# A hybrid encoder trunk: TensorE's order of the first stage, from a priority scheduler to a planned, tied weave

## The chip, the cores and the metric

The kernel runs on one core of a Trainium2 chip. A core has five engines with a queue of instructions each: TensorE (PE in the profile; its weight loads stand apart as PEld), VectorE (DVE), ScalarE (ACT), GpSimd (POOL) and SyncE (SP), which here only issues DMAs. The order of each queue is fixed when the program is built; what an instruction has to wait for is told by semaphores. The metric is the device time of one execution in microseconds, lower is better.

## What is computed

A two-layer encoder on 1024 frames of width 1024, all in float32. The part that the change touches is layer 0's mixer: one projection whose columns feed eight RWKV-7 heads and eight heads of chunked band attention.

```python
def rwkv_attention_mixer(h, w_in, mu, ..., rel_bias, w_out):
    proj = h @ w_in
    p_rwkv, q, k, v = jnp.split(proj, [...], axis=-1)
    y_rwkv = rwkv7_group(p_rwkv, mu, ...)
    y_att = chunk_band_attention(q, k, v, rel_bias)
    return jnp.concatenate([y_rwkv, y_att], axis=-1) @ w_out

def step(S, inp):                       # the RWKV recurrence, frame by frame
    r_t, w_t, k_t, v_t, kk_t, a_t = inp
    sa = jnp.einsum('bhij,bhj->bhi', S, -kk_t)
    S = (S * w_t[:, :, None, :] + sa[..., None] * (kk_t * a_t)[:, :, None, :]
         + v_t[..., None] * k_t[:, :, None, :])
    y = jnp.einsum('bhij,bhj->bhi', S, r_t)

for layer in range(DEPTH):              # DEPTH = 2
    h = rmsnorm(x, mix_norms[layer])
    x = x + (rwkv_attention_mixer(h, ...) if layer % 2 == 0 else conformer_conv(h, ...))
    x = x + sq_relu_mlp(rmsnorm(x, g_ffn), up, down)
```

## The kernel before

**Dense work.** Activations lie with channels on the 128 partitions and 512 frames (one half `h` of the sequence) in the free dimension. A dense step multiplies a 128x128 weight tile with a 128x512 tile. Float32 operands are split into a high and a low part, and three matmuls (lines 270 to 272) take the place of one: high by high, high by low, low by high. One output tile takes 8 x 3 of them. In the order of the program the dense work is: `w_in` for half 0, `w_in` for half 1, `w_out` and layer 0's MLP for half 0, and then layer 1 and the rest. The weights are loaded by SP, cast by ACT (214) and subtracted by DVE (215), under the priority "support".

**RWKV.** The recurrence is made in chunks of 64 frames. A unit is two heads by 256 frames (four chunks); there are 8 units for each half, 16 in all. `prep` mixes r, k and v from the projections that were written to DRAM, makes decays, normalises k (sums over heads at 439, spread back at 446) and forms the chunk matrices `g` by eight matmuls of 64x128 tiles (546), masked by DVE (549). The diagonal 16x16 blocks of `g` then have to be inverted. They are gathered by eight small DMAs into DRAM (`msc`, 557) and two back (`nb`, 562), DVE inverts them in about twenty short steps (574 to 585), two DMAs write the result (`xsc`, 592), eight read it back as diagonal blocks (`xdt`, 599), and DVE transposes them (605). The first matmul that uses that is 611; three more rounds (623) make the inverses of the whole chunks. `stacks` transposes operands (640, 645), `chain` carries the state through the four chunks with three dependent matmuls each (668, 672, 678), every one followed by copies on DVE and ACT, and `finish` normalises the output (702 to 720). Below, "the inversion loop" is what lies between a unit's last matmul of 546 and the end of its transpose 605.

**Attention.** For each pair of heads and each tile of 128 queries: scores (797, 799), softmax on DVE and ACT (801 to 810), transposes (819), and probabilities by values (826).

**What sets the order.** The kernel emits these streams one after the other under priorities (`At("support")` first, then "mixer", "attn", "dense"), and a list scheduler at build time places each engine's instructions by priority among what it takes to be ready. So TensorE's dense steps fill what the streams leave. The RWKV and attention of half 0 share TensorE with `w_in` of half 1, those of half 1 with `w_out` and the MLP of half 0. PSUM, TensorE's output memory, is parted into `d` (2 banks, dense), `w` (2), `v` (1), `c` (1, the chain) and `a` (2, attention).

Of the kernel before, what the change touches and what calls it, by code (L numbers as in the profile page):

```python
# [14 lines left out]
P = 128  # L15
# [38 lines left out]
LINE = 32  # L54

# [6 lines left out]
def encoder_trunk(ctx: ExitStack, tc: tile.TileContext, x, vecs, consts, ext, w2a2, g2, w_in, w_out,  # L62
# [15 lines left out]
    deferred = []  # L78

    def psum(tag):  # L80
        return ps[tag].tile([P, T], F32, tag=tag, name=tag)

# [68 lines left out]

    def tmp(tag="t1"):
        return dpool.tile([P, T], F32, tag=tag, name=tag)
# [16 lines left out]
    class Stat:  # L170
# [12 lines left out]
        def sums(self, eps_col=0):  # L183
            q = psum("o" if wide[0] and self.ps == "d" else self.ps)
            with At("dense") if wide[0] else nullcontext():
                for j in range(4):
                    nc.tensor.matmul(q[:, j : j + 1], self.acc[:, j * P : (j + 1) * P], ones[:, 0:1], start=True, stop=True)
# [6 lines left out]
        def spread(self):  # L194
            q, c = self.part
            with At("dense") if wide[0] else nullcontext():
                for j in range(4):
                    nc.tensor.transpose(q[:, j * P : (j + 1) * P], c[:, j : j + 1].to_broadcast([P, P]), ident)
            self.r = self.pool.tile([P, T], F32, tag=self.pre + "rstd", name="rstd", bufs=1)
            nc.scalar.copy(self.r[:], q[:])  # L200
# [22 lines left out]
    def gemm(w, row0, mts, rhs, evac, st=None, first=(), taper=False, after=None, halves=False):  # L223
# [28 lines left out]
        for i, (grp, cols) in enumerate(units):  # L252
# [3 lines left out]
            for k in range(KT):  # L256
# [10 lines left out]
                with At("dense"):  # L267
                    for q, parts in zip(qs, ws):
                        hi, lo = (a[:, k % KH, :] for a in parts[k // KH])
                        nc.tensor.matmul(q[:, cols], hi, xh[:, cols], start=(k == 0), stop=False)  # L270
                        nc.tensor.matmul(q[:, cols], hi, xl[:, cols], start=False, stop=False)  # L271
                        nc.tensor.matmul(q[:, cols], lo, xh[:, cols], start=False, stop=(k == KT - 1))  # L272
# [6 lines left out]
            if after is not None:  # L279
                late_m += [(m, cols) for m in grp]  # L280
        if late_m:
            deferred.append(tail)

    IN_ORDER = [12, 13] + [t for j in range(4) for t in (j, 4 + j, 8 + j)] + list(range(14, 22))


    def load_x(h, xrp, out=None):
# [17 lines left out]
        for k in range(KT):  # L305
            q = psum("w" if k % 2 else "a") if h == 0 else psum("w")
            for t in range(4):
                nc.tensor.transpose(q[:, t * P : (t + 1) * P], raws[t][:, k * P : (k + 1) * P], ident)
# [26 lines left out]
    def w_in_gemm(h, rhs, st, first=()):  # L335
        def evac(m, q, cols):
# [14 lines left out]
            else:  # L351
                nc.gpsimd.dma_start(pd[m][:, ts], s[:])

        gemm(w_in, 0, IN_ORDER, rhs, evac, st, first)
        qs = [psum(tag) for tag in SPARE]
        for k in range(KT):
            with boost():
                hi, lo = (a[:].rearrange("p a b -> p (a b)")
                          for a in weight_part(w_in[k * P : (k + 1) * P, V0 * P : V0 * P + RW], RW))
            xh, xl = rhs[k]  # L360
            with At("dense"):
                for t, q in enumerate(qs):
                    ts = slice(t * P, (t + 1) * P)
                    nc.tensor.matmul(q[:], xh[:, ts], hi, start=(k == 0), stop=False)
                    nc.tensor.matmul(q[:], xl[:, ts], hi, start=False, stop=False)
                    nc.tensor.matmul(q[:], xh[:, ts], lo, start=False, stop=(k == KT - 1))
        with boost():
            for t, q in enumerate(qs):
                s = tmp("t1")
                nc.scalar.activation(s[:], q[:], AF.Copy, scale=st.part[1][:, t : t + 1])  # L370
                nc.gpsimd.dma_start(vd[h * T + t * P : h * T + (t + 1) * P, :], s[:])


    def rwkv(h, rp, nbuf):
# [12 lines left out]
        for i in range(n + 2):  # L387
            gens = []
            if i >= 2:
                gens.append(units[i - 2][2]())  # L390
            if 1 <= i <= n:
                gens.append(units[i - 1][1]())
            if i < n:
                gens.append(units[i][0]())
            while gens:
                for g in list(gens):
                    try:
                        next(g)
                    except StopIteration:
                        gens.remove(g)  # L400

    def rwkv_block(tb, rp, nbuf, keep):
# [28 lines left out]
        def vbank():  # L431
            return psum("v")[:, 0:RT]
# [4 lines left out]
        def head_sums(q, src):  # L437
            for b in range(RT // P):
                nc.tensor.matmul(q[:, 2 * b : 2 * b + 2], src[:, b * P : (b + 1) * P], bones[:, 0 : C + 1 : C],
# [3 lines left out]
        def head_spread(q, r, wide):  # L443
            nc.scalar.copy(wide[:].rearrange("p (h c) -> p h c", c=C), r[:].unsqueeze(2).to_broadcast([P, 4, C]))
            for b in range(RT // P):
                nc.tensor.transpose(q[:, b * P : (b + 1) * P], wide[:, b * P : (b + 1) * P], ident)
# [16 lines left out]
        def prep(hp, u):  # L463
            if not lora_in:
                shared()
                yield
# [5 lines left out]
            vp = rp.tile([P, RT + 2 * C], F32, tag="vp", name="vp", bufs=nbuf - 1)  # L472
            nc.gpsimd.memset(vp[:, 0:C], 0.0)
            nc.gpsimd.memset(vp[:, RT + C : RT + 2 * C], 0.0)
            mix(8 + hp, vp[:, C : RT + C])
            yield
            wps = rbank()
            aps = rbank()
            for i, q in enumerate((wps, aps)):
                nc.tensor.matmul(q, lora[i][:, cs], lora_in[i][:], start=True, stop=False)  # L480
                nc.tensor.matmul(q, lora[2 + i][:, cs], lora_in[i][:], start=False, stop=True)
# [14 lines left out]
            yield  # L496
            ksq = e()
            nc.scalar.activation(ksq[:], k[:], AF.Square, scale=v("k_k", hp))
            sps = rbank()
            inv = head_sums(sps, ksq)  # L500
            nc.scalar.activation(inv[:], sps[:, 0:4], AF.Sqrt)
            nc.vector.tensor_scalar(inv[:], inv[:], 1e-12, None, op0=ALU.max)
            nc.vector.reciprocal(out=inv[:], in_=inv[:])
            yield
            head_spread(sps, inv, e())
            yield
# [21 lines left out]
            yield  # L528
# [4 lines left out]
            nc.tensor.matmul(bps, bones, bon[:], start=True, stop=True)  # L533
            bv = rp.tile([P, RT], F32, tag="bv", name="bv", bufs=nbuf)
            nc.vector.tensor_tensor(out=bv[:], in0=bps, in1=vp[:, C : RT + C], op=ALU.mult)

            yield
            g = rp.tile([P, NCH, 2, 2, C], F32, tag="g", name="g", bufs=nbuf)
            mask = con("mask").rearrange("p (k t) -> p k t", k=2).unsqueeze(1).to_broadcast([P, 4, 2, C])
            for q4 in range(NCH // 4):  # L540
                mb = [bank(), bank()]
                for j in range(4):
                    c = 4 * q4 + j
                    for hd in range(2):
                        s = slice(64 * hd, 64 * hd + 64)
                        nc.tensor.matmul(mb[hd][:, j * P : (j + 1) * P], bk[s, c, :], ar[s, c, :],  # L546
# [18 lines left out]
            u.update(hp=hp, g=g, ar=ar, bk=bk, vp=vp, dc=dc, bv=bv, nb=nb)  # L565

        def invert(u):
            hp, g, nb = u["hp"], u["g"], u["nb"]
# [10 lines left out]
            for r in range(8):  # L579
# [7 lines left out]
                if r == 4:  # L587
                    yield
            xsc = dram.tile([2, 16, 16, 16], F32, tag=f"xsc{tb}{hp}", name="xsc")
            x0 = xsc[:]  # L590
            for hd in range(2):
                nc.sync.dma_start(bass.AP(tensor=x0.tensor, offset=x0.offset + 4096 * hd,
                                          ap=[[64, 4], [256, 16], [1, 64]]),
                                  xi[C * hd : C * hd + C, :, :].rearrange("p a b -> p (a b)"))
            xd16 = keep["xdt"]
# [11 lines left out]
            hs = [slice(0, C), slice(C, P)]  # L607
            tq = vbank()
            for c in range(NCH):
                for hd, s in enumerate(hs):  # L610
                    nc.tensor.matmul(tq[s, c * C : c * C + C], g[s, c, 0, hd, :], xn[s, c * C : c * C + C],
                                     start=True, stop=True)
            yield
# [5 lines left out]
            for i in range(3):  # L619
                uq = vbank()  # L620
                for c in range(NCH):
                    for s in hs:
                        nc.tensor.matmul(uq[s, c * C : c * C + C], at[s, c * C : c * C + C], rhs[s, c, :],  # L623
                                         start=True, stop=True)
                yield
                if i < 2:
                    rhs = blk(e("e2", 2)[:])
                    nc.vector.tensor_tensor(out=rhs, in0=blk(uq), in1=xd16, op=ALU.add)
            xt = u["xt"] = keep["xt", hp % 2]
            for hd, s in enumerate(hs):  # L630
                nc.vector.tensor_tensor(out=xt[s, :, hd, :], in0=blk(uq)[s, :, :], in1=xd16[s, :, :], op=ALU.add)

# [544 lines left out]
```

## Time and profile before

| | |
|---|---|
| median of three timed runs | 2471.99 us (2471.95 to 2474.72) |
| the profiled execution | 2471.67 us |
| its span, first to last instruction | 2469.9 us |
| TensorE busy / weight loads / DVE / ACT / POOL | 99% / 80% / 69% / 49% / 5% of the span |
| mean granted TensorE clock | 0.998 |
| last matmul of the RWKV and attention streams starts at | 872.8 us |
| matmul rows in the trace | 12828 |

The profile comes from one execution. A row of a timeline has the start in us, the duration in us, the engine, the line, the operation with its output tile and its inputs, shapes, a count where equal rows were merged, and in brackets how long the engine had been idle and what ended that. Matmuls overlap: a dense matmul lasts 0.39 us from its start to its end, and the next one starts 0.23 us after it. So TensorE counts as busy while it waits for less than the overlap, and starts of neighbouring rows say more than busy shares. A float32 matmul that is not split or a transpose shows as two rows; the program has 11338 matmuls for those 12828 rows. Every line number in these rows is that of the kernel before; in the kernel after, all matmuls have the line of a helper, and are told apart by the names of their tiles.

### The profile page before, as it was taken

To read this page: it belongs to the slowest core of one execution; us is meant where nothing else is said; L and a number is where in the kernel's file an instruction comes from. 1 tells how busy PE (TensorE), PEld (TensorE's weight loads), DVE (VectorE), ACT (ScalarE), POOL (GpSimd) and SP (SyncE) were. 2 spreads that over 40 slices of the span, in tenths; PEclk is the share of its full clock that TensorE was granted. 3 is DMA by queue.
4 is the path that set the end of the run, shared out by engine and by line. 5 is a ranking of instruction groups with operands and counts; after the bars stand their busy time and mean duration, and the time that the engine had idled before them with its cause. 6 is when DMAs were issued, how large, how long until landed. Compare 5 with 4: busy or idle time off the path is not lost.

```text
span 2469.9 us, 37195 instructions
## 1 busy us (share of the span) xinstructions
PE 2436.1 (99%) x12828; PEld 1967.3 (80%) x12828; DVE 1715.7 (69%) x3575; ACT 1199.1 (49%) x2308; POOL 114.0 (5%) x283
## 2 busy tenths in 40 slices
PE   8999999999999999999999999999999999999998
PEld 6777777777777788888888888888888888888887
DVE  5688875688877534459999946599998475444444
ACT  5557766577766733343443235434432365433334
POOL 1110111100000000001000000000000000000000
PEclk9999999999999999999999999999999999999999
DMA  8554434643233233373333333533333334333332
GB/s 270 169 151 129 129 104 137 204 116 104 84 105 92 75 96 95 99 213 95 95 96 100 95 98 93 163 98 95 94 95 101 94 103 149 99 94 97 100 94 69
DMA packets 476460, 283.36 MB, mean 115 GB/s; under 512 B 44512, under 2 KB 453472, under 8 KB 476272
## 3 DMA queue, kind: packets, MB, share of 16 engines
q1 hardware_dynamic: 466080, 250.25, 34.9%
q0 software_dynamic: 9152, 29.36, 3.3%
q8 instruction: 101, 1.65, 0.3%
q10 hardware_dynamic: 1040, 1.38, 0.2%
q14 instruction: 87, 0.71, 0.1%
HBM read 247.31 MB, written 36.72 MB: 115 GB/s over the span
## 4 chain that ended last, share of the span: by engine, by line
PE 91%; DVE 3%; DMA 3%; ACT 2%; issue 1%; SPq 0%; ACTq 0%; DVEq 0%
PE d L270 25%; PE d L271 25%; PE d L272 25%; PE a L826 2%; PE w L546 1%; PE v L623 1%; PE a L819 1%; PE a L797 1%; PE c L678 1%; PE c L668 1%; DVE wl L215 1%; PE c L672 1%; DMA pt<-pd 1%; PE a L799 1%; DMA nb<-msc 1%
## 5 line engine op out<-in xcount | busy, mean ns | idle before, releaser
L214 ACT CAST wh<-wr 128x512 fp32r<-128x512 f32 x744 | 461.0, 621 | 949.9 <-PE d L271 866.2
L270 PE MATMUL d<-xh,wh 128*128 128x512 f32 x1872 | 741.9, 396 | 0.5 <-ACT wh L214 0.5
L272 PE MATMUL d<-xh,wl 128*128 128x512 f32 x1872 | 738.3, 395 | 0.9 <-DVE wl L215 0.9
L271 PE MATMUL d<-xl,wh 128*128 128x512 f32 x1872 | 739.2, 395 | 0.0
L215 DVE TENSOR_TENSOR wl<-wr,wh 128x512 fp32r<-128x512 f32 x744 | 503.1, 687 | 218.6 <-ACT wh L214 165.2
L272 PEld LDWEIGHTS d<-xh,wl 128*128 128x128 f32 x1872 | 352.8, 188 | 70.8 <-DVE wl L215 1.6
L270 PEld LDWEIGHTS d<-xh,wh 128*128 128x128 f32 x1872 | 352.8, 189 | 70.4 <-issue 1.3
L271 PEld LDWEIGHTS d<-xl,wh 128*128 128x128 f32 x1872 | 353.1, 189 | 68.5 <-issue 1.2
L270 PE MATMUL d<-mh,wh 128*128 128x512 f32 (+1 forms) x1040 | 403.7, 388 | 0.0
L271 PE MATMUL d<-ml,wh 128*128 128x512 f32 (+1 forms) x1040 | 403.5, 388 | 0.0
L272 PE MATMUL d<-mh,wl 128*128 128x512 f32 (+1 forms) x1040 | 403.2, 388 | 0.0
L949 DVE SCALAR_TENSOR_TENSOR cv<-u,dwt,cv 128x512 f32<-128x512 f32 x480 | 333.1, 751 | 0.7
L270 PEld LDWEIGHTS d<-mh,wh 128*128 128x128 f32 x1040 | 195.6, 188 | 38.1 <-issue 0.2
L272 PEld LDWEIGHTS d<-mh,wl 128*128 128x128 f32 x1040 | 195.5, 188 | 38.2
L271 PEld LDWEIGHTS d<-ml,wh 128*128 128x128 f32 x1040 | 195.4, 188 | 38.1
L848 DVE TENSOR_TENSOR x<-d,x 128x512 f32<-128x512 f32 (+1 forms) x146 | 97.8, 682 | 154.7 <-PE d L272 154.5
L890 DVE SCALAR_TENSOR_TENSOR t<-d,rstd 128x512 f32<-128x512 f32 x128 | 86.6, 689 | 114.9 <-PE d L272 112.2
L896 DVE TENSOR_TENSOR ml<-t,mh 128x512 fp32r<-128x512 f32 x128 | 88.1, 690 | 20.7 <-ACT mh L894 18.0
L892 ACT ACTIVATE t<-t 128x512 f32<-128x512 f32 x128 | 80.1, 626 | 15.8 <-DVE t L890 15.2
L894 ACT ACTIVATE mh<-t 128x512 fp32r<-128x512 f32 x128 | 78.9, 616 | 0.0
L181 DVE TENSOR_TENSOR acc<-acc,t 128x512 f32<-128x512 f32 (+1 forms) x86 | 58.0, 675 | 9.0 <-ACT t L180 8.7
L677 ACT ACTIVATE sd<-vs,dc 64x64 f32<-64x64 f32 x128 | 44.2, 345 | 31.2 <-DVE vs L681 23.3
(273 smaller groups left out, 2407.3 us busy)
## 6 DMA issues: line engine op xcount, KB each, us to landing
wr<-in_up_dram SPq DMA_DIRECT2D x256, 256.0 KB
wr<-in_dn_dram SPq DMA_DIRECT2D x256, 256.0 KB
wr<-in_w_in_dram SPq DMA_DIRECT2D x104, 256.0 KB
wr<-in_pw_dram SPq DMA_DIRECT2D x96, 256.0 KB
wr<-in_w_out_dram SPq DMA_DIRECT2D x32, 256.0 KB
pd<-t POOLq DMA_DIRECT2D x28, 256.0 KB, 2.6
x<-xd SPq DMA_DIRECT2D x24, 256.0 KB
pt<-pd SPq DMA_DIRECT2D x42, 128.5 KB
```

The source lines that it names most:

```text
L181: nc.vector.tensor_tensor(out=self.acc[:, cols], in0=self.acc[:, cols], in1=sq[:, cols], op=ALU.add)
L214: nc.scalar.copy(hi[:], raw[:])
L215: nc.vector.tensor_tensor(out=lo[:], in0=raw[:], in1=hi[:].bitcast(F32), op=ALU.subtract)
L270: nc.tensor.matmul(q[:, cols], hi, xh[:, cols], start=(k == 0), stop=False)
L271: nc.tensor.matmul(q[:, cols], hi, xl[:, cols], start=False, stop=False)
L272: nc.tensor.matmul(q[:, cols], lo, xh[:, cols], start=False, stop=(k == KT - 1))
L848: nc.vector.tensor_tensor(out=xs[m][:, cols], in0=q[:, cols], in1=xs[m][:, cols], op=ALU.add)
L890: nc.vector.scalar_tensor_tensor(out=t[:], in0=q[:], scalar=0.0, in1=rstd[:], op0=ALU.max, op1=ALU.mult)
L892: nc.scalar.activation(sq[:], t[:], AF.Square)
L894: nc.scalar.activation(hi[:], t[:], AF.Square)
L896: nc.vector.tensor_tensor(out=lo[:], in0=sq[:], in1=hi[:].bitcast(F32), op=ALU.subtract)
L949: nc.vector.scalar_tensor_tensor(out=c[:], in0=u[:, tap : tap + T], scalar=dw(tap), in1=c[:], op0=ALU.mult, op1=ALU.add)
```

## The change

TensorE's order in the stage that holds RWKV and attention is no longer found by the scheduler. Every matmul goes through a helper that adds a nominal duration to a planned clock, `pe["now"]`, and, while `strict` is on, ties the instruction to the one before it by a dependency that costs no semaphore and only fixes the order. The dense work becomes a generator that yields after every group of three matmuls. RWKV's `prep`, `invert`, `stacks`, `chain` and `finish` and the attention become five plus one jobs, each a generator that yields a `Need`: so many planned us after now, so many free `w` banks, perhaps a condition on another job. `weave` takes a dense group, and then lets every job go whose need is met on the planned clock; `drain` runs the jobs without dense work.

With it come smaller edits. PSUM's `v` bank joins `w` (3 banks). The inversion's DVE steps and its `xsc` DMAs move from `invert` into the end of `prep`, and `invert` begins with the `xdt` DMAs; its first matmul stands at least 25 planned us after the unit's `g` matmuls. In `prep` the sums for k's norm come before the decays, and v is loaded later. The second transposes of `stacks` become eight 64-column matmuls with an identity, and the transpose and copy of line 602 go. Half 0's `w_in` is split: five tiles before, then three tiles, the value part, and the rest in another order within the weave. Outside of the weave (layer 1 and on) the same work is emitted as before.

```diff
+    pe = {"now": 0.0, "last": None, "strict": False, "w": [0.0] * 3, "held": [], "shape": None}
...
+    def issued(ins, us, shape):
+        pe["now"] += us + (SWITCH if shape != pe["shape"] else 0.0)
+        pe["shape"] = shape
+        if pe["strict"]:
+            if pe["last"] is not None:
+                tc.add_manual_dep(ins.ins, pe["last"].name,
+                                  mybir.DependencyInfo(mybir.DependencyClass.NoSync, mybir.DependencyReason.DATA),
+                                  reason="order of TensorE")
+            pe["last"] = ins.ins
...
+    class Job:
...
+        def ready(self):
+            w = self.want
+            if w.cond is not None:
+                if not w.cond():
+                    return False
+                self.want = w = Need(w.after, w.shape, w.banks, None, w.hold)
+                self.at = max(self.at, pe["now"] + w.after)
+            return pe["now"] >= self.at and sum(t <= pe["now"] for t in pe["w"]) >= w.banks
...
+    def weave(dense, jobs):
+
+        pe["strict"] = True
+        value = None
+        while True:
+            if all(j.done for j in jobs):
+                pe["strict"] = False
+            try:
+                next(dense)
+            except StopIteration as e:
+                value = e.value
+                break
+            pump(jobs)
+        return value
...
+        return [
+            Job("mixer", job("chain", lambda i, hp: was("invert", i) and was("stacks", i)), lead=True),
+            Job("mixer", job("stacks", lambda i, hp: was("prep", i) and was("chain", i - (nbuf - 1)))),
+            Job("mixer", job("invert", lambda i, hp: was("prep", i))),
+            Job("mixer", job("prep", lambda i, hp: all((h, m) in have for m in srcs(hp)))),
+            Job("mixer", job("finish", lambda i, hp: was("chain", i))),
+        ]
...
-            u.update(hp=hp, g=g, ar=ar, bk=bk, vp=vp, dc=dc, bv=bv, nb=nb)
-
-        def invert(u):
-            hp, g, nb = u["hp"], u["g"], u["nb"]
...
+            u.update(hp=hp, g=g, ar=ar, bk=bk, vp=vp, dc=dc, bv=bv, xsc=xsc, made=pe["now"])
+
+        def invert(u, ui, was):
+            hp, g, xsc = u["hp"], u["g"], u["xsc"]
...
-            vl = psum("v")[:, 0:P]
-            nc.tensor.transpose(vl, u["vp"][:, NCH * C : NCH * C + P], ident)
-            nc.scalar.copy(u["vs"][:, :, 1, NCH - 1, :], vl[:, C:P].unsqueeze(1).to_broadcast([P, 2, C]))
...
+            yield Need(max(6.5, u["made"] + 25.0 - pe["now"]), 1, 1)
...
-        def chain(u):
+        def chain(u, ui, was):
+            link = 2.1
...
-                nc.tensor.matmul(zp, g[:, c, 0, :, :].rearrange("p h t -> p (h t)"), sv[:, :, c, :], start=True, stop=True)
+                matmul(zp, g[:, c, 0, :, :].rearrange("p h t -> p (h t)"), sv[:, :, c, :], start=True, stop=True)
...
+                yield Need(link)
...
+            jobs.append(Job("attn", attention(0, ap)))
+
+            def dense():
+                yield from w_in_gemm(0, ra, sa)
+                for what in w_in_gemm(1, reload_x(1, lp), sb):
+                    if what == "value":
+                        drain(jobs, jobs[-1:])
+                    yield
+
+            weave(dense(), jobs)
+            drain(jobs)
```

**TensorE, where the inversion loop ends.** These are rows of TensorE's order around the first matmuls that use a unit's inverse (the row with `g` and 64x64), for the fifth unit. `d` is a dense output, `c` the chain's bank, `a` attention's, `v` and `w` the other streams' banks. Before:

```order
L270 MATMUL d<-xh,wh 128x512
L271 MATMUL d<-xl,wh 128x512
L272 MATMUL d<-xh,wl 128x512
L611 MATMUL v<-e_2661,g 64x64 x8
L439 MATMUL w<-cst,e 128x2 x2
```

And now:

```order
L105 MATMUL d<-xh,wl 128x512
L105 MATMUL c<-zs,xt_682 128x64
L105 MATMUL w<-e_3406,g 64x64 x8
L105 MATMUL d<-xh,wh 128x512
L105 MATMUL d<-xl,wh 128x512
L105 MATMUL d<-xh,wl 128x512
L105 MATMUL w<-ar,bk 128x128 x8
```

The streams now stand between groups of exactly three dense matmuls. What moved is the distance: between a unit's last `w<-ar,bk` matmul and its first with `g` and 64x64 there stood 62 to 140 dense matmuls before, 96 in the mean of the 16 units (82 for this one), and now 54 to 96, 70 in the mean (72 for this one). All matmuls counted, it was 149 to 232 and is 107 to 145. Over the whole program, neighbours of different kinds (split dense work or not, another size of the array's tile) were 1045 and are 872.

**DVE, where the inversion starts.** These are DVE's rows from the masks of the first unit (`g<-w,cst`) to the first step of its inversion (`fold<-nb`), with `wl` a weight's low part. Before:

```order
L549 TENSOR_TENSOR g<-w,cst 128x8x64 x2
L422 SCALAR_TENSOR_TENSOR vp<-pt,vec,e 128x256
L663 COPY vs<-sfin 64x64 x2
L343 TENSOR_TENSOR t_776<-d,rstd 128x512
L215 TENSOR_TENSOR wl<-wr,wh 128x512
L490 SCALAR_TENSOR_TENSOR dx<-wx,cst 128x260
L493 RECIPROCAL e<-dx 128x256
```

Now:

```order
L684 TENSOR_TENSOR g<-w,cst 128x8x64 x2
L324 TENSOR_TENSOR wl<-wr,wh 128x512
L799 COPY vs<-sfin 64x64 x2
L614 TENSOR_SCALAR hs<-hs 128x4
L615 RECIPROCAL hs<-hs 128x4
L324 TENSOR_TENSOR wl<-wr,wh 128x512 x2
L705 TENSOR_TENSOR fold<-nb 128x128
```

Before, five more rows follow until that unit's `fold<-nb`, so that eleven lie between; now five do. From a unit's masks to its transpose 605, DVE has 92 instructions in the mean of the 16 units before (68 to 109) and 65 now (50 to 76); with the median duration of each kind in the trace of before these are 35.0 and 24.5 us of DVE work. Of that, what stands from `fold<-nb` to the last step of the inversion is 16.1 us before and 11.7 us now (7.0 to 15.9).

More of the change, by code (lines that the diff above doesn't have):

```diff
@@ L54 @@
 LINE = 32
+PER_COL = 0.443e-3
+SWITCH = 0.09
 def whole(n):
@@ new lines, in encoder_trunk, with __init__, pump, open_ @@
+    class Need:
+        def __init__(self, after, shape=0, banks=0, cond=None, hold=1.4):
+            self.after, self.shape, self.banks, self.cond, self.hold = after, shape, banks, cond, hold
+    def pump(jobs, force=False):
+        def open_():
+            return [j for j in jobs if not j.done and j.ready()]
+        some = open_()
+        if not some:
+            return False
+        if not force and not any(j.lead for j in some):
+            soon = any(j.lead and not j.done and j.want.cond is None and j.at - pe["now"] < 1.4 for j in jobs)
+            if soon and all(pe["now"] - j.at < 2.0 for j in some):
+                return False
+        free = sum(t <= pe["now"] for t in pe["w"])
+        take = []
+        for j in some:
+            if j.want.banks <= free:
+                free -= j.want.banks
+                take.append(j)
+        for j in sorted(take, key=lambda j: j.want.shape):
+            j.go()
+        return True
@@ new lines, in weave, with drain @@
+    def weave(dense, jobs):
[4 more added lines that the diff above has]
+                pe["strict"] = False
+            try:
+                next(dense)
[4 more added lines that the diff above has]
+        return value
+    def drain(jobs, some=None):
+        while not all(j.done for j in some or jobs):
+            if not pump(jobs, True):
+                pe["now"] += 0.1
@@ L152, in tmp, with run @@
+    def run(gen):
+        while True:
+            try:
+                next(gen)
+            except StopIteration as e:
+                return e.value
     def tmp(tag="t1"):
@@ L352, in evac, with value_part @@
                 nc.gpsimd.dma_start(pd[m][:, ts], s[:])
[L354 to L361, printed above, removed]
+            have.add((h, m))
+        def value_part():
+            qs = [psum(tag) for tag in SPARE]
+            for k in range(KT):
+                with boost():
+                    hi, lo = (a[:].rearrange("p a b -> p (a b)")
+                              for a in weight_part(w_in[k * P : (k + 1) * P, V0 * P : V0 * P + RW], RW))
+                xh, xl = rhs[k]
@@ new lines, in value_part @@
+                    yield
+            with boost():
+                for t, q in enumerate(qs):
+                    s = tmp("t1")
+                    nc.scalar.activation(s[:], q[:], AF.Copy, scale=st.part[1][:, t : t + 1])
+                    nc.gpsimd.dma_start(vd[h * T + t * P : h * T + (t + 1) * P, :], s[:])
+            ready_v.add(h)
+        if ahead:
+            yield from gemm(w_in, 0, ahead, rhs, evac, st, first)
+            return
+        if h == 0:
+            yield from gemm(w_in, 0, IN_ORDER[5:8], rhs, evac, st)
+            yield from value_part()
+            yield from gemm(w_in, 0, LATE_ORDER, rhs, evac, st)
+        else:
+            yield from gemm(w_in, 0, IN_ORDER, rhs, evac, st)
+            yield "value"
+            yield from value_part()
@@ L386, in rwkv, with job @@
         n = len(units)
[L387 to L400, printed above, removed]
+        done = set()
+        was = lambda what, i: i < 0 or (what, i) in done
+        def job(what, cond):
+            for i in range(n):
+                hp = i % 4
+                yield Need(0.0, 0, 0, lambda: cond(i, hp))
+                yield from units[i][what](i, was)
+                done.add((what, i))
+        srcs = lambda hp: [12, 13, hp, 4 + hp, 8 + hp]
+        return [
[5 more added lines that the diff above has]
+        ]
     def rwkv_block(tb, rp, nbuf, keep):
@@ L618, in invert @@
             rhs = xd16
-            for i in range(3):
+            for j in range(3):
+                yield Need(1.8, 1, 1, (lambda: was("chain", ui - 2)) if j == 2 else None)
                 uq = vbank()
@@ L853, in evac @@
                 last(m, cols)
-        gemm(w, row0, range(KT), rhs, evac, taper=taper, after=after, halves=halves)
+        yield from gemm(w, row0, range(KT), rhs, evac, taper=taper, after=after, halves=halves)
     def norm_collect(xs, gname):
@@ L935, in evac @@
                 us[j] = u
-        gemm(pw1, 0, [m for j in range(KT) for m in (j, KT + j)], rhs, evac, st)
+        yield from gemm(pw1, 0, [m for j in range(KT) for m in (j, KT + j)], rhs, evac, st)
         return us
```

253 lines of the change are left out of this document (145 added, 108 removed).

## The prediction

> **What bounds the kernel now.** I read the windows first, to see which stage has anything to give.
>
> ```profile
> 100.00:450.00 350.00, 346.60 (x2393) 262.51 (x2392) 262.29 (x793) 229.99 (x522) 42.26 (x102) 1.00 0.44 131
> 450.00:880.00 430.00, 421.89 (x2952) 327.11 (x2951) 321.00 (x967) 301.60 (x641) 29.43 (x92) 1.00 0.38 109
> 880.00:2470.00 1590.00, 1581.19 (x7090) 1310.62 (x7088) 1076.79 (x1715) 614.74 (x1049) 26.59 (x32) 1.00 0.36 105
> ```
>
> The columns are the window, its length, and the busy time and rows of PE, PEld, DVE, ACT and POOL, then the granted clock. From 880 us on TensorE runs dense work alone; nothing there is touched. In the two windows before it, which hold RWKV and attention, TensorE is idle for 350 - 346.60 + 430 - 421.89 = 11.5 us. So the kernel is bound by TensorE from end to end, and whatever makes TensorE wait or work longer in the woven stage is added to the end, one for one. Busy time hides short waits, though, so I went on to the starts of neighbouring rows, in TensorE's timeline.
>
> ```profile
> 603.39 0.33 PE L819 MATMUL a<-cst,pt 128*128 128x128 f32 x1
> 603.48 0.49 PE L271 MATMUL d<-xl,wh 128*128 128x512 f32 x1
> 603.80 0.60 PE L819 MATMUL a<-cst,pt 128*128 128x128 f32 x4
> 604.16 0.47 PE L272 MATMUL d<-xh,wl 128*128 128x512 f32 x1
> 604.47 0.39 PE L270 MATMUL d<-xh,wh 128*128 128x512 f32 x1
> 604.70 0.39 PE L271 MATMUL d<-xl,wh 128*128 128x512 f32 x1
> ```
>
> A dense matmul behind another one takes 0.23 us (604.47 to 604.70). Behind a transpose it takes 0.31 to 0.32 (603.48 to 603.80, 604.16 to 604.47). **A change of kind costs 0.09 us.** If every row of the two windows is given the usual step of its shape and of its neighbours' kinds, the 2393 + 2952 rows come to 736 us of the 780: TensorE waits there for 44 us at the most, and for 11.5 at the least.
>
> Then I looked for the wait that the change makes tight, and took the quickest of the 16 inversion loops, that of the last unit. TensorE, DVE and SP, each from its own timeline:
>
> ```profile
> 785.67 0.93 PE L546 MATMUL w<-ar,bk 64*128 64x128 f32 x6
> 816.92 0.68 PE L611 MATMUL v<-e,g 64*64 64x64 f32 x16
> ```
>
> ```profile
> 786.64 0.69 DVE L549 TENSOR_TENSOR g<-w,cst 128x512 f32<-128x512 f32 x1 [1.96 <-PE w L546]
> 794.92 0.38 DVE L574 TENSOR_TENSOR fold<-nb 128x128 f32<-128x128 f32 x1 [0.70 <-DMA nb<-msc]
> 803.71 0.29 DVE L585 TENSOR_REDUCE xi<-pr 128x8 f32<-128x128 f32 x1
> 815.76 0.45 DVE L605 STREAM_TRANSPOSE e<-xdt 128x256 f32<-128x256 f32 x1
> ```
>
> ```profile
> 784.36 4.71 SPq L557 DMA_DIRECT2D msc<-g  x8
> 791.73 0.56 SPq L562 DMA_DIRECT2D nb<-msc  x1
> 804.02 1.18 SPq L592 DMA_DIRECT2D xsc<-xi  x2
> 806.74 2.75 SPq L599 DMA_DIRECT2D xdt<-xsc  x6
> 811.48 0.97 SPq L599 DMA_DIRECT2D xdt<-xsc  x2
> ```
>
> The last matmul of `g` starts at 786.3, the masked `g` is there at 787.3, the gathered blocks 7.6 us later (DVE waited for their DMA at 794.92), the inversion ends at 804.0, and the transpose at 816.2. That is **29.9 us** with nothing wasted but DVE's queue. Another unit, the eighth:
>
> ```profile
> 346.49 1.16 PE L546 MATMUL w<-ar,bk 64*128 64x128 f32 x8
> 383.50 0.45 DVE L605 STREAM_TRANSPOSE e<-xdt 128x256 f32<-128x256 f32 x1
> ```
>
> Its last matmul starts at 347.4 and its transpose ends at 383.9, 36.6 us. Over the 16 units (the first ends at 131.4, the last is the one above) it is 29.9 to 48.6 us, 38.6 in the mean. TensorE hardly waits for it before:
>
> ```profile
> L611 PE MATMUL v<-e,g 64*64 64x64 f32 x256 | 11.2, 224 | 1.9 <-DVE e L605 1.5 <-DVE st L809 0.2
> L672 PE MATMUL c<-zs,xt 128*128 128x64 f32 x128 | 24.8, 275 | 1.3 <-ACT zs L671 0.8
> ```
>
> The group of 611 shows 1.9 us of idle time in all, since the scheduler put it 96 dense matmuls behind `g`. The new order puts it 70 behind.
>
> **The change part by part.** I add up against the profiled execution, 2471.67 us (span 2469.9 and 1.8 around it), which is the median of the timed runs to 0.4 us.
>
> Changes of kind: 1045 become 872, 173 x 0.09 = 15.6 us less. The 16 transposes of 602 go too, at about 0.1 each between dense steps; the eight narrow matmuls that replace four transposes in `stacks` I take for equal. Together **-17 us**, all on the path, since TensorE is the bound.
>
> Waits of the old order: between 11.5 and 44 us stand there. The links of the chain give an idea of what the plan can save. In a quick one TensorE comes back 1.4 us later:
>
> ```profile
> 845.85 0.38 PE L668 MATMUL c<-vs,g 128*128 128x128 f32 x2
> 847.22 0.43 PE L672 MATMUL c<-zs,xt 128*128 128x64 f32 x2 [0.30 <-ACT zs L671]
> ```
>
> The plan asks for 2.1 us, nine dense steps. That covers a quick link, but not one whose copy stands behind 0.7 us operations on DVE and ACT. So I let **24 us** of the 44 go, and keep 20. The other waits stated (2.4 in `finish`, 4.5 before the spread, 8 before the bonus) are of the same sort and are in this term.
>
> The inversion loop: between the last `g` matmul and the first use stand, in the new order, 54 to 96 dense matmuls and 11 to 85 others. For the last unit: 96 x 0.227 = 21.8, eleven chain matmuls for about 2.0 (0.2 each, 0.1 for the narrow ones), and the kind changes' 23 x 0.09, part of which the small rows' overlap gives back: 25 us. Done so for all 16 it is 22.5 to 26.6, 24.8 in the mean. So the planned 25 us are what TensorE has to do there, if nothing else waits. The loop needs: 1.0 to mask, 7.6 to gather, the inversion, and 8.5 or more to return. The last is from SP's rows, two `xsc` issues 1.2, 1.5 until the first lands, eight `xdt` issues, then their landing and the transpose.
>
> ```profile
> L599 SPq DMA_DIRECT2D xdt<-xsc x128: 303/424/1879, 121.8 to 812.0; - x128
> ```
>
> The row gives minimum, median and maximum of an issue: 8 x 0.424 = 3.4, and with landing (about 2, as from `xsc` to `xdt`) and 0.45 for the transpose 8.5. The inversion is 11.7 us of DVE work in the new order (other streams' steps stand between); in the old one 16.1 us of work took 14.9 us, so 10.8. Sum 1.0 + 7.6 + 10.8 + 8.5 = 27.9, and 29 with some of SP's queue. **TensorE waits 29 - 24.8, about 4 us.** What is queued behind: all of TensorE, for its order is tied, dense steps too, and so DVE's evacuations and, through the weights' buffers, SP. For two units the wait of the one before falls into their own room, so 14 x 4 = **+56 us**. The ends: none, if the loop shrinks to 25; (38.6 - 24.8) x 16 = 220 if it stays as slow as before. I take the value near the quickest row, since DVE's work in the loop falls from 35.0 to 24.5 us.
>
> The clock: this shows what follows a wait of that size.
>
> ```profile
> 69.77 0.39 PE L270 MATMUL d<-xh,wh 128*128 128x512 f32 x1
> 74.31 0.55 PE L480 MATMUL w<-xl,lora 128*128 128x256 f32 x1 [4.15 <-DVE xl L461]
> 75.73 0.63 PE L272 MATMUL d<-xh,wl 128*128 128x512 f32 x1
> 76.15 0.63 PE L270 MATMUL d<-xh,wh 128*128 128x512 f32 x1
> 79.99 0.41 PE L270 MATMUL d<-xh,wh 128*128 128x512 f32 x1
> 80.25 0.39 PE L271 MATMUL d<-xl,wh 128*128 128x512 f32 x1
> ```
>
> ```profile
> 75.00:80.00 5.00, 5.00 (x15) 3.94 (x14) 2.02 (x5) 0.92 (x3) 0.82 (x3) 0.50 0.59 181
> ```
>
> After 4.15 us of idle time TensorE has half its clock until about 80: a dense step takes 0.43 instead of 0.23, ten of them lose 2 us, and 2.3 with the small ones ahead. Seven of the 16 loops come out with waits over 4 us, so 7 x 2.3 = **+16 us**.
>
> The Trainium skill, "TensorE: Matmul & The Clock Gate", section "Why this matters for your kernels", asks for no idle gap over about 3 us between bursts, since a window of idleness halves the clock. The trace agrees for 4.15 us. By that rule taken strictly, 14 waits instead of 7 would pay, 16 us more; by the row alone the sum stands as it is. It speaks against tying all of TensorE to one late operand.
>
> Sum: -17 - 24 + 56 + 16 = +31, so 2471.67 + 31 = **2503 us**.
>
> **The rivals.** *The loop fits its room* (the plan works). It needs 25 us instead of 29: that takes an inversion of 7 us, as five of the 16 orders on DVE allow (7.0 to 8.7 us of work), in all units. Then only -17 and -11.5 to -44 are left, 2411 to 2443; with 10 us for new short waits, 2440. This ends faster, and it decides at a loop of about 27 us, where the waits (14 x 2 = 28, with no clock loss) still leave -13. For it speaks that DVE's queue is shorter; against it the DMA parts, 16 us of SP issues and landings that the change doesn't shorten.
>
> *Gain and wait cancel*: a loop of 27.5 to 28, 14 x 3 = 42 against 41; 2472. The chain waits less long then, and no clock is lost.
>
> *The loop stays long*: SP's in-order queue holds weights that wait for buffers between `xsc` and `xdt` (at 811.48 two `xdt` issues stand 2 us behind the six others). At 33 us the wait is 8.2, x 15 = 123, plus 15 x 2.3 = 34, less 41: 2588.
>
> That the order isn't what the plan says is excluded: the rows of the new order stand in groups of three dense matmuls.
>
> **How the numbers follow.** Forecast (loop waits, 2480 to 2540): 0.52. Loop fits: 0.28. Cancel: 0.11. Long: 0.09. The range that leaves out 2 in 10 drops the lower third of the second case and most of the last: 2432 to 2555. The forecast alone would be 2480 to 2540. A change of 0.2%, 5 us, is about what a measurement of this kernel can tell from none. Faster: 0.28 and a little of the cancelling case, 0.30; same 0.09; slower 0.61.
>
> **What would show it.** In the profile after, the group with output `w`, inputs `e,g` and 64x64 should head TensorE's idle times, with some 50 us, ended by the transpose on DVE, and the granted clock in 100 to 880 should fall below 1.00. The rows from the last `w<-ar,bk` to that group should show 28 to 30 us. The chain's three groups should keep their idle times or lose some. If that group has under 10 us, the loop step is wrong, and the time is near 2440. If other groups head the idle times (loads of `pt`, softmax), I missed a wait. A second stage that is longer than 1590 us from the last stream's matmul on would contradict the claim that nothing there is touched.

## The result, and the profile after

The changed kernel takes **2595.1 us** (median of four runs, 2590.9 to 2597.3) where the kernel before took 2472.0 (2471.3 to 2474.7) on the same chip: a ratio of 1.049, 95% interval 1.048 to 1.051. It is slower by 123 us. The direction was forecast, the size was not: 2503 was predicted and the range ended at 2555.

From the page of the kernel after, the busy times and the granted clock in 40 slices:

```profile
PE 2434.3 (94%) x13004; PEld 1992.5 (77%) x13004; DVE 1717.5 (66%) x3575; ACT 1203.7 (46%) x2294; POOL 107.0 (4%) x251
PEclk9988899999999999999999999999999999999999
```

The windows of the kernel after, with the columns of the windows before:

```profile
100.00:450.00 350.00, 295.75 (x2067) 235.34 (x2067) 227.96 (x669) 195.17 (x424) 33.97 (x82) 0.92 0.40 117
450.00:880.00 430.00, 375.37 (x2540) 304.81 (x2536) 270.06 (x780) 260.42 (x536) 26.87 (x65) 0.94 0.36 106
880.00:1000.00 120.00, 105.66 (x784) 85.89 (x783) 80.18 (x252) 75.95 (x157) 4.73 (x13) 0.99 0.30 85
1000.00:1200.00 200.00, 192.17 (x1056) 156.40 (x1057) 101.07 (x203) 77.58 (x153) 6.40 (x18) 0.99 0.33 95
1200.00:2590.00 1390.00, 1386.13 (x6230) 1149.16 (x6228) 988.55 (x1583) 544.30 (x935) 21.32 (x27) 1.00 0.35 104
```

In the two windows up to 880 us TensorE now idles 54.3 + 54.6 = 109 us, where it was 11.5, and starts 4607 rows instead of 5345. The streams no longer end there: their last matmul starts at 1113.4 us instead of 872.8, and from 880 to 1200 us TensorE idles another 14.3 + 7.8 = 22 us. Over the whole span it idles 2595.1 - 2434.3 = 161 us, where it was 34. The clock is granted at 0.92 and 0.94 instead of 1.00, worth at most 0.08 x 350 + 0.06 x 430 = 54 us of TensorE's time, part of which it idled anyway. No other engine is busier in these two windows: DVE and ACT are busy for less time too. From 1200 us on, nothing is lost. So TensorE waits, and the view of TensorE's waits in the kernel after says for what (the line after the arrow is the releaser's; then total, times, longest):

```profile
PE a L109 <- ACT pt L953: 36.9, 14, 6.3
PE w L105 <- DVE e L735: 23.1, 9, 5.9
PE c L105 <- DVE sfin L819: 17.4, 16, 2.3
PE a L109 <- ACT pT L964: 12.8, 4, 6.3
PE a L105 <- DVE st L944: 9.6, 5, 5.4
PE w L105 <- ACT e L610: 8.5, 1, 8.5
PE c L105 <- ACT zs L807: 6.9, 9, 2.4
```

The groups of TensorE in the kernel after (busy, mean ns of one, then the idle time ahead and its releasers) say the same:

```profile
L109 PE MATMUL a<-cst,pt 128*128 128x128 f32 x240 | 42.6, 301 | 49.7 <-ACT pt L953 36.9 <-ACT pT L964 12.8
L105 PE MATMUL w<-e,g 64*64 64x64 f32 x256 | 11.8, 236 | 23.1 <-DVE e L735 23.1
```

The inversion (`e`, 735) stands second with 23.1 us. First is the softmax, which the prediction's sum didn't price: 36.9 + 12.8 us ahead of the transposes of the probabilities. Third is the state's update (819), behind which the change states no wait after the chain's last chunk.

How the waits hang together is seen in one inversion loop of the kernel after, that of the eleventh unit. TensorE:

```profile
730.28 1.16 PE L105 MATMUL w<-ar,bk 64*128 64x128 f32 x16
...
742.42 0.27 PE L105 MATMUL a<-kk,ql 128*128 128x128 f32 x1
...
747.79 0.74 PE L109 MATMUL a<-cst,pt 128*128 128x128 f32 x5
...
750.23 0.39 PE L105 MATMUL d<-mh,wl 128*128 128x512 f32 x1
756.94 1.33 PE L109 MATMUL a<-cst,pt 128*128 128x128 f32 x5 [6.32 <-ACT pT L964]
757.92 0.78 PE L105 MATMUL d<-mh,wh 128*128 128x512 f32 x1
758.50 0.63 PE L105 MATMUL d<-ml,wh 128*128 128x512 f32 x1
758.92 0.63 PE L105 MATMUL d<-mh,wl 128*128 128x512 f32 x1
...
764.21 0.68 PE L105 MATMUL w<-e,g 64*64 64x64 f32 x16
```

The last `g` matmul starts at 731.2 and the first use at 764.2, 33.0 us later. There TensorE waits for nothing, though the loop is 8 us longer than its planned 25: it has stood for 6.3 us at five transposes on the way, and then runs dense steps of 0.42 us (758.50 to 758.92) where the steps ahead of the stop took 0.23. One stop has served two late operands. DVE, ACT and SP in the same stretch, each from its own timeline:

```profile
742.41 0.28 DVE L705 TENSOR_TENSOR fold<-nb 128x128 f32<-128x128 f32 x1
747.04 0.29 DVE L944 CUSTOM_DVE_ANT_0 pt<-a,bias 128x128 f32<-128x128 f32 x1
749.39 0.14 DVE L950 TENSOR_SCALAR st<-st 128x1 f32<-128x1 f32 x1
752.93 0.29 DVE L716 TENSOR_REDUCE xi<-pr 128x8 f32<-128x128 f32 x1
761.44 0.44 DVE L735 STREAM_TRANSPOSE e<-xdt 128x256 f32<-128x256 f32 x1
```

```profile
751.18 1.28 ACT L951 ACT_TABLE_LOAD   x1
752.48 0.83 ACT L951 ACTIVATE pt<-pt,st 128x640 f32<-128x640 f32 x1
753.72 0.83 ACT L953 ACTIVATE pt<-pt,st 128x640 f32<-128x640 f32 x1
756.32 0.57 ACT L964 COPY pT<-a 128x512 f32<-128x512 f32 x1
```

```profile
736.86 0.57 SPq L697 DMA_DIRECT2D nb<-msc  x1
738.76 0.56 SPq L697 DMA_DIRECT2D nb<-msc  x1
753.25 1.18 SPq L721 DMA_DIRECT2D xsc<-xi  x2
755.10 3.61 SPq L732 DMA_DIRECT2D xdt<-xsc  x8
```

The last scores of that tile's second head start at 742.4. DVE takes them at 747.0, since steps of another unit's `prep`, the inversion's own and two of the dense work stand in its queue; the maximum is there at 749.5; ACT, after other streams' work, loads a table and takes the exponential at 752.5; the copy of the first head's transposes (964), which ends TensorE's wait, stands behind all that on ACT and starts at 756.3, 8 us after those transposes. The plan states 1.6 us between them and the second head's. No operation in these two queues lasts over 1.3 us on the way. The planner counts only TensorE's own durations, and a queue like this isn't in the waits it states.

The loop's own parts here: 731.2 to 742.4 for mask and gather (SP's last issue of `nb` is done at 739.3, and the first step on it starts 3.1 us later), to 753.2 for the inversion, to 761.9 for the way back (SP issues until 758.7). Over the 16 units the means are 12.0, 10.3 and 10.1 us, 32.4 together, and the way from `g` to the first use is 29.5 to 37.8 us, 33.2 in the mean.

### The profile page after: what moved, and what is told of

Its sections match the earlier page's. It is cut to its first block, busy times and chain, and to the rows that moved or that the text cites. A ratio compares the mean times of both kernels' runs of the same rounds, so it can differ in the third digit from the quotient of the medians.

```text
span 2595.1 us, 37406 instructions
## 1 busy us (share of the span) xinstructions
PE 2434.3 (94%) x13004; PEld 1992.5 (77%) x13004; DVE 1717.5 (66%) x3575; ACT 1203.7 (46%) x2294; POOL 107.0 (4%) x251
## 3 DMA queue, kind: packets, MB, share of 16 engines
q1 hardware_dynamic: 466080, 250.25, 33.2%
## 4 chain that ended last, share of the span: by engine, by line
PE 59%; DVE 0%; ACT 0%; issue 0%; ACTq 0%; DVEq 0%
PE d L105 58%; PE o L109 0%; PE w L105 0%; PE c L105 0%; PE o L105 0%; PE w L109 0%; DVE wl L324 0%; ACT u L1169 0%; DVE t L1035 0%; DVE sfin L819 0%; ACT t L1037 0%; ACT wh L323 0%; ACTq L1330 0%; ACT mh L1039 0%; DVE x L993 0%
## 5 line engine op out<-in xcount | busy, mean ns | idle before, releaser
L105 PE MATMUL d<-xh,wh 128*128 128x512 f32 x1872 | 768.0, 410 | 1.3 <-ACT wh L323 1.3
L105 PEld LDWEIGHTS d<-xh,wl 128*128 128x128 f32 x1872 | 358.0, 191 | 79.6 <-DVE wl L324 1.8
L105 PEld LDWEIGHTS d<-xh,wh 128*128 128x128 f32 x1872 | 359.0, 192 | 77.9 <-issue 4.7
L105 PE MATMUL d<-mh,wh 128*128 128x512 f32 (+1 forms) x1040 | 411.8, 396 | 0.0
L105 PEld LDWEIGHTS d<-xl,wh 128*128 128x128 f32 x1872 | 359.1, 192 | 65.6 <-issue 0.5
L109 PE MATMUL a<-cst,pt 128*128 128x128 f32 x240 | 42.6, 301 | 49.7 <-ACT pt L953 36.9
L109 PEld LDWEIGHTS a<-cst,pt 128*128 128x128 f32 x240 | 31.0, 156 | 57.8 <-ACT pt L953 41.1
```

The lines of the kernel that those rows point to most:

```text
L105: issued(nc.tensor.matmul(out, lhs, rhs, **kw), max(cols, 0.1 if m == P else 0.06), (lhs.shape[0], m, n == T))
L109: issued(nc.tensor.transpose(out, src, idn), 0.11, (P, P, False))
```

## The experiments

Two theories stood at the start. **A**, the prediction's: the inversion loop carries the loss. **B**: the attention's waits, which head the list, carry it. Later came **L** (the loop again, with its measured 33.2 us, and the other stops only the same time met earlier) and **S**: many stated waits are too short, they run side by side, and each hides the others. All kernels have the changed program unless an edit says otherwise. "Tied" means that an instruction keeps the planner's place in TensorE's queue; one that isn't tied gets its place from the scheduler.

| run | what is tied, which waits | us, median | against before, 95% |
|---|---|---|---|
| the change | all | 2595.1 | 1.048 to 1.051 |
| e1 | nothing | 2464.7 | 0.995 to 0.998 |
| e2 | dense, RWKV | 2598.6 | 1.049 to 1.052 |
| e3 | dense, attention | 2573.5 | 1.040 to 1.043 |
| e4 | all; a wait after the chain's last chunk | 2594.2 | 1.048 to 1.051 |
| e5 | all; inversion 33 | 2567.6 | 1.037 to 1.040 |
| e6 | all; softmax 8 | 2606.6 | 1.050 to 1.056 |
| e7 | all; the edits of e4, e5, e6 together | 2548.6 | 1.029 to 1.032 |
| e8 | RWKV, attention; dense free | 2486.5 | 1.004 to 1.007 |
| e9 | dense, RWKV; inversion 33, e4's wait | 2526.1 | 1.021 to 1.024 |
| e10 | nothing; the edits of e7 | 2479.3 | 1.002 to 1.004 |
| e11 | RWKV, attention; the edits of e7 | 2473.9 | 1.000 to 1.002 |
| e12 | dense, inversion | 2525.4 | 1.020 to 1.023 |
| e13 | dense, attention; softmax 8 | 2559.3 | 1.034 to 1.037 |
| e14 | dense, RWKV without the inversion | 2546.5 | 1.029 to 1.032 |

### e1: no tie

```diff
-        pe["strict"] = True
+        pe["strict"] = False
```

> The new program with its emission, but TensorE's instructions are not tied to one order: the scheduler places them by priority, as before. If the tie (fixed places and stated waits that are too short) makes the loss, almost all of it goes: 2465 to 2490 us. If the loss is in what else the change does (streams begun later, value part moved, smaller edits), it stays: 2560 us or more. By the prediction's own theory (the inversion loop under a tie) it goes as well, to about 2455 to 2475.

2464.7 us. All of the loss goes with the tie; everything else that the change does is worth -0.34% (0.2 to 0.5%). The edit does a little more than its line says: the same flag also switches on the planner's count of free `w` banks (in `psum`), so e1 and e10 hand over their matmuls in a somewhat different order. No run separates that; e8 keeps the count and still comes within 22 us of e1. e1 is the only version that is faster than both kernels. Its page, windows and groups:

```profile
PE 2417.2 (98%) x13004; PEld 1954.9 (79%) x13004; DVE 1711.3 (69%) x3575; ACT 1191.9 (48%) x2288; POOL 107.4 (4%) x251
100.00:450.00 350.00, 342.13 (x2469) 262.77 (x2469) 258.79 (x781) 224.26 (x498) 42.38 (x96) 1.00 0.47 137
450.00:880.00 430.00, 419.87 (x3078) 325.44 (x3077) 324.67 (x979) 301.60 (x642) 25.02 (x65) 1.00 0.38 109
```

```profile
L109 PE MATMUL a<-cst,pt 128*128 128x128 f32 x240 | 42.2, 284 | 0.9 <-ACT pt L953 0.2 <-ACT pT L964 0.2
L105 PE MATMUL w<-e,g 64*64 64x64 f32 x256 | 10.9, 224 | 1.9 <-DVE e L735 1.0 <-DVE st L952 0.6
```

The clock is at 1.00, and the two groups wait 2.8 us where they waited 72.8 (49.7 + 23.1) in the change. Yet the loops are no shorter: 30.0 to 45.9 us, 35.8 in the mean. So the tie doesn't slow the loops. The scheduler puts more work into them, about 24 more dense matmuls in the mean.

### e2 and e3: attention alone, or RWKV alone, out of the tie

```diff
-        if pe["strict"]:
+        if pe["strict"] and pe["job"] not in ('attn',):     # e3: ('mixer',)
...
                     hold = self.want.hold
+                    pe["job"] = self.name
...
+                finally:
+                    pe["job"] = None
```

Outside of a job, in the dense steps, the name is `None`.

> Only the attention's TensorE instructions are left out of the tie; dense steps and RWKV stay tied as in the change. Theory A (the prediction's: the inversion loop's waits and their cold clock carry the loss): little goes, 2570 to 2600 us. Theory B (the attention's stated waits, above all the one from softmax to the transposes, carry most; 78 us of late starts in the trace and half of the cold clock): 2490 to 2520 us. If the waits only move to the next tied operand, 2540 to 2570.

> Only RWKV's TensorE instructions (preparation, inversion, stacks, chain, finish) are left out of the tie; dense steps and attention stay tied. Theory A: nearly all the loss goes, 2470 to 2500 us. Theory B: the attention's 78 us stay, with their share of the cold clock, and about 70 us of RWKV's late starts go: 2520 to 2550 us.

Neither theory stands. Without the attention's tie nothing is gained (2598.6), so B falls; without RWKV's only 22 us are (2573.5), so A falls, and e3 is above B's range too. The groups of e2 show where the time went:

```profile
L109 PE MATMUL a<-cst,pt 128*128 128x128 f32 x240 | 43.0, 297 | 11.0 <-ACT pt L956 10.0 <-ACT pT L967 0.7
L105 PE MATMUL w<-e,g 64*64 64x64 f32 x256 | 14.8, 276 | 53.5 <-DVE e L738 50.7 <-DVE st L953 2.8
```

The transposes' wait fell by 38.7 us (49.7 to 11.0) and the inversion's rose by 30.4 (23.1 to 53.5). Taking the largest entry of the list of waits out of the tie gained nothing, though the attention tied without RWKV costs 2573.5 - 2464.7 = 109 us.

### e4: a wait where the list shows one in 16 of 16 chains

```diff
-                if c < NCH - 1:
-                    yield Need(link)
+                yield Need(link)
```

> One more stated wait: the chain gives way for 2.1 us after its last chunk too, before the outputs' matmuls, as it does after the others. The trace shows 17.4 us of TensorE idle time there in 16 places, so 17 to 25 us should go: 2570 to 2578 us. By theory A, which puts the loss into the inversion loop, those 16 waits only shift, and the time stays within 2588 to 2600.

2594.2: nothing. The 17.4 us are gone from the list of e4's waits, and the softmax has taken up part:

```profile
PE a L109 <- ACT pt L952: 43.0, 15, 7.8
PE w L105 <- DVE e L735: 26.2, 8, 5.0
```

### e5, e6, e7: longer stated waits

```diff
-            yield Need(max(6.5, u["made"] + 25.0 - pe["now"]), 1, 1)
+            yield Need(max(6.5, u["made"] + 33.0 - pe["now"]), 1, 1)     # e5, e7
...
-                    yield Need(4.6 if hd == 0 else 1.6)
+                    yield Need(8.0 if hd == 0 else 1.6)                  # e6, e7
```

> The inversion's stated wait is 33 planned us instead of 25, all else as in the change; the plan itself now idles 5.5 us at one place. Theory L (the loop from the last matmul of g to its first use lasts 33.2 us in the mean and its room is 24.8; what TensorE idles at other waits inside the loop is only the same 8 us met earlier): about 14 x 8 = 112 us go, 2485 to 2515 us. Theory S (the attention's and the chain's short waits hold TensorE up by themselves and cover the loop; each alone would cost nearly the same): 2560 to 2600.

> The stated wait from the second head's scores to the first head's transposes is 8 planned us instead of 4.6; the plan idles 10.5 us at one place. Theory L: nothing goes, the loops still lack their room: 2590 to 2612 us. Theory B (the softmax wait carries its 54 us of late starts): 2540 to 2565.

> Inversion 33 planned us, softmax 8, and the chain's wait after its last chunk; the plan idles 20 us. Theory L: as with the inversion's 33 alone and the plan's 15 us more idle time on top, 2500 to 2530 us. Theory S (parallel limits): only now the loss goes, 2490 to 2530, while either alone stays above 2560. If the loops grow along with their room, because the plan's TensorE time isn't what they wait for, 2560 or more.

L falls with e5. The loops got their room: the transpose ends 33.1 us after `g` in the mean, and TensorE comes back at 39.2. Only 27 us of the 112 went. The waits in e5:

```profile
PE a L109 <- ACT pt L953: 32.6, 9, 9.1
PE c L105 <- DVE sfin L819: 21.0, 16, 4.6
PE a L105 <- DVE st L944: 10.9, 4, 5.4
```

The softmax and the chain hold TensorE up by themselves. e6 gained nothing, as L said and B didn't; its four runs lie from 2591 to 2608 us, wider than the others'. e7 gained 46 us and ends above the ranges of L and of S and below that of growing loops: other waits are left, and the plan itself idles 20 us there, since longer waits make the streams of half 0 too long for the dense work beside them.

### e8 and e11: only the dense steps out of the tie

```diff
+        if pe["strict"] and pe["job"] not in (None,):
```

> RWKV's and the attention's TensorE instructions stay tied among themselves in the plan's order, and only the dense steps are left out of the tie. If the loss is dense work that stands behind a late small instruction, nearly all of it goes: 2465 to 2500 us. If the small streams delay one another, and the dense steps run out while they wait: 2520 to 2570.

> Dense steps not tied, the small streams tied among themselves, with the longer waits (inversion 33, softmax 8, chain after its last chunk). Theory S: the 21 us by which the version with the short waits stands behind the untied one come from small streams that delay one another, and the longer waits take some of them away: 2465 to 2480 us. If what the dense steps did was only to fill, it stays at 2483 to 2490.

2486.5: with the small streams in the planner's order among themselves, and only the dense steps free, 109 of the 130 us come back. The loss is dense work that stands behind a late small instruction. The longer waits give 12.6 us more (e11, as S expected), to the time of the kernel before.

### e9: the loop's room and the attention's freedom together

> The attention's TensorE instructions are left out of the tie, the inversion's stated wait is 33 planned us, and the chain gives way after its last chunk too. One by one these brought +3.5, -27.5 and -1 us against the change's 2595. If the effects add up: about 2570. Theory S (several waits stated too short run side by side, each hides the others, and time goes only when all of them get room): clearly more than the sum, 2490 to 2535 us.

2526.1. One by one the edits (those of e2, e5 and e4) brought +3.5, -27.5 and -0.9 us; together they bring -69. This is S's reading, and addition (2570) is ruled out.

### e10: longer waits without the tie

> Nothing tied, and the new program's stated waits longer (inversion 33, softmax 8, chain after its last chunk), which here change only the order in which the program hands its instructions to the scheduler. If the scheduler's own times set the order and the stated waits hardly matter without the tie: 2458 to 2472 us, as with the tie off alone (2464.7). If the stated waits shape the order there too, some us less: 2445 to 2458.

2479.3, 14.6 us slower than e1 and outside of both expectations. Without the tie the stated waits still set in which order the program hands over its instructions. Why the longer ones are worse there was not tried.

### e12, e14, e13: each part alone

The inversion got a job name of its own, so that it could be tied without the rest of RWKV.

```diff
+        if pe["strict"] and pe["job"] not in ('attn', 'mixer'):     # e12; e14: ('attn', 'invert')
...
+        jobs[2].tag = "invert"
```

> Only dense steps and the inversion's own TensorE instructions are tied to the plan's order (stated wait 25 as in the change); attention, preparation, stacks, chain and finish are free. It measures the inversion loop by itself, against the untied program's 2464.7. The prediction's size for it (14 waits of 4 us and a cold clock after seven, 72 us): about 2537. Theory L (16 loops of 33 us in 25 us of room, 115 to 130 us): 2575 to 2595. Theory S: each wait alone is a limit of nearly the full size, so 2530 to 2580 too. If one tied stream costs little as long as the others are free to fill: 2465 to 2490.

> Dense steps, preparation, stacks, chain and finish tied to the plan's order; the inversion and the attention free. The prediction gave these waits no loss but put them into a gain of 24 us: by it about 2440 to 2470. If the effects of RWKV's parts add up: 2464.7 and 134 less 61, about 2538. If each part alone costs nearly as much as all (parallel limits): 2540 to 2600.

> As with RWKV untied (2573.5: dense steps and attention tied), but the stated wait before the first head's transposes is 8 planned us instead of 4.6; the plan idles 10 us at one place. If the softmax wait, which the prediction didn't price, makes the attention's loss: 25 us or more go, 2530 to 2550. If other waits of the attention make it (loads of keys and queries, the outputs' wait, the scores), or if each hides the others there too: 2560 to 2590.

Against e1 the inversion alone costs 61 us, near the prediction's 72; L's 115 is out, and S's lower end is missed by 5. The likeness of the sums hides different parts. TensorE's waits in e12 show 22 us in eight stops for the late transpose, where 14 stops and 56 us were predicted:

```profile
PE w L105 <- DVE e L741: 22.3, 8, 6.7
```

By the pages of e12 and e1, TensorE idles 41 us more (85.9 against 45.1) and is busy 22 us longer with the same 13004 rows (2439.5 against 2417.2).

The rest of RWKV alone costs 82, a little more than the 73 that addition would leave it (134 less 61). Of the attention's 109 (e3) a longer softmax wait takes 14 away (e13), 10 us of the plan's own idle time already paid; 2559.3 lies just under the second of the two expected ranges. It isn't the softmax alone. In the groups of e14, where the inversion is free, it is waited for again, beside the chain:

```profile
L105 PE MATMUL w<-e,g 64*64 64x64 f32 x256 | 12.0, 238 | 20.5 <-DVE e L741 19.6 <-DVE zs L812 0.5 <-DVE st L958 0.4
L105 PE MATMUL c<-ar,vs 64*64 64x64 f32 x256 | 11.3, 230 | 13.5 <-DVE sfin L825 13.4
```

## Why the prediction was wrong

**The cause, as the runs show it.** Tied to the dense steps, the inversion costs 61 us, the rest of RWKV 82, the attention 109: 252 together, if they added up. All tied cost 130. RWKV's two parts nearly do add up (143 against 134 for all of RWKV, e2); what hides is RWKV and the attention behind each other (134 + 109 against 130). While TensorE stands at one late operand, DVE, ACT and SP go on with what the other streams wait for, so one stop pays for several. This fits that taking away one wait brought nothing (e2, e4, e6) or 27 us (e5), and three edits together brought 69 (e9). That each stop is shared in this way was read in one loop's rows and is otherwise argued from these sums.

**The step that failed** is the term "waits of the old order". It let 24 us go and said of the other stated waits that they "are of the same sort and are in this term". They are no gain. RWKV's other waits cost 82 us by themselves (e14), and the attention's, which the sum nowhere had, cost 109 (e3). The prediction looked at one quick link of the chain (1.4 us, against 2.1 stated), said that slower links aren't covered, and still booked a gain for all of these waits. There is no term in it that sets a stated wait of the attention against what the softmax takes, with DVE's and ACT's queues before it.

**The loop.** The mechanism was right: DVE's transpose late, and all of TensorE behind it. That the sum came near, 61 us alone (e12) where 56 + 16 were predicted, is in part luck: the wait for the transpose itself was 22 us there and not 56. The room, 24.8 us, was about right: of the 33.2 us from `g` to the first use TensorE idles 6.4 in the mean, and at most 2.4 more are lost to the clock. The length was mis-sized: 32.4 us to the transpose's end instead of 29. Mask and gather took 12.0 us in the mean, where 8.6 had been taken from the quickest of the 16 loops; the inversion on DVE took 10.3 for the predicted 10.8. The way back took 10.1, where 8.5 had been put together from single issues and a landing. No loop of the kernel before shows so short a way back: its rows give 9.9 to 20.9 us, and 12.2 (804.0 to 816.2) in the very loop that the prediction shows. The prediction also expected this group to head the idle times with some 50 us. It has 23.1, since TensorE stopped earlier on the way, and 53.5 where the attention no longer stops it (e2).

**The rivals.** "The loop stays long" had 33 us and 2588, close to 2595, but it isn't the explanation: with 33 us of room the loss was still 95 us (e5). Its reason, SP's queue, doesn't show either: in the 16 loops of the change SP goes from its last `xsc` issue to its first of `xdt` within 0.7 to 2.4 us. "The loop fits its room" and "gain and wait cancel" are out. The sentence that other groups at the head of the idle times would mean a missed wait is what came true.

**The clock.** It fell below 1.00 between 100 and 880, as expected, and a stop of 6.3 us is followed by steps of 0.42 instead of 0.23 us. The 16 us were for seven stops of the loop alone; the windows up to 880 allow up to 54. With the same 13004 rows TensorE is busy 2434.3 us in the change and 2417.2 in e1, 17 more, and idles 161 instead of 45. So most of the loss is idle time. The 17 us are an estimate, since other things differ in the two orders as well.

**Changes of kind**, -17 us: no run measures it by itself. e1, with the same edits in the scheduler's order, gains 7 us; TensorE is busy 19 us less there than before (2417.2 against 2436.1) and idle 11 us more. How much of the 19 are changes of kind isn't shown.

**The second stage** is as it was: 1200 to 2590 us with TensorE busy and a clock of 1.00. From the last stream's matmul to the end it is 1482 us, under the 1590 that the prediction named as a limit.

## What to carry to other kernels

An order that is fixed by one engine's own durations makes every late operand a stop for everything behind it. Price each stated wait against the slow cases of the profile, with the queues of the engines between (above, 1.6 us were stated and the copy came after 8), and leave the work that has no deadline out of the fixed order: the dense steps alone, set free, gave 109 of 130 us back. When many waits are short at once, the list of waits doesn't rank causes; set one stream after the other free, and also tie each one alone.
